# Two-block transformer step on one core: the last residual, norm, transposes and first feed-forward products by token tiles, the last stores by 512 columns

## The chip, the cores and the metric

The kernel runs as one program on one core of a Trainium2 chip. The metric is the device time of one execution in microseconds (us). The engines are named as in the profile: PE (TensorE, with PEld for its weight loads), DVE (VectorE), ACT (ScalarE), POOL (GpSimd) and SP (SyncE, which issues most DMAs). Each engine executes its own instructions in order; waits on other engines go by semaphores.

## The reference, cut to what matters

A first block (a recurrent mixer, a dense feed-forward, a block attention and a mixture of experts) runs on 256 tokens of width 1024, and its result x enters a second block of two layers, modulated by a condition c. In layer 1, the last, the mixer is a latent attention whose result is projected by `od_w_o` (1024 x 1024). The part that the change touches is the end of that layer:

```python
def modulate(h, shift, scale):
    return h * (1 + scale) + shift

def conv_ffn(h, w_up, conv_w, conv_b, w_down):      # w_up 1024 x 5632, w_down 2816 x 1024
    u = dwconv_centred(h @ w_up, conv_w, conv_b)     # over 3 neighbouring tokens
    a, g = jnp.split(u, 2, axis=-1)
    return (a * jax.nn.silu(g)) @ w_down
...
        yx, yc = odd_mixer(...)                      # ends in (...) @ w_o
        x = x + g1 * rms_norm(yx, norm_g[l, 1])
        hx = modulate(rms_norm(x, norm_g[l, 2]), sh2, sc2)
        x = x + g2 * rms_norm(conv_ffn(hx, ffn_w_up[l], ...), norm_g[l, 3])
    return x
```

All weights and activations are float32.

## The kernel before

**Tiles.** The 256 tokens are two token tiles of 128 (`tb` 0 and 1). A matrix lies either by tokens (tokens on the 128 partitions, `h`, `ypr`, `ffy`) or transposed (128 of the 1024 features on the partitions, all 256 tokens along the row, 8 blocks k, as `hT0h`). `h` is the residual stream, `ypr` the output projection's result, `ffy` first the normed rows and later the feed-forward's result.

**Products.** A float32 product is made of three products in the format f32r: each operand is split in a high part (suffix h, `whi`) and the rest (suffix l, `wlo`), and high by high, low by high and high by low are summed in PSUM (`mm`, L312). `wload` brings a weight panel by DMA into `wraw` (six buffers), ACT copies it to `whi` (L297) and DVE subtracts for `wlo` (L300, 128x512 at a time).

**Stages.** Generators yield after each step and a scheduler, which also orders the instructions of each engine, interleaves them. `x_chain` runs layer 1 in this order: `mla_x` (attention), `out_proj`, `modulated`, `ffn_conv`, and with its end the program ends.

- `lin_tok` (L378 and following) multiplies by tokens, 512 columns of the result at a time, with operand `omla` for the projection. In the last column block it holds back the last two groups of weights and finishes tile 0 before tile 1; after tile 0 it calls `late()`, by which `gate_row` makes the gate vector `gcol` into a row on all partitions (`brow`).
- `residual` (L1453) runs after the whole projection, for tile 0 and then tile 1: squares of `ypr` on ACT (`sq`), the sum (`ss`) and the scale (`rp`) on DVE, the root on POOL (`rs`, L343), two products with the gate row, and two `stt` (L309) of 512 columns that add to `h`.
- `modulated` (L1428) works out `scale` and `shift` (8 columns each), norms both tiles to `ffy` (`inv_rms` and L304), and calls `to_T`. That transposes on PE, 16 pieces of 128x128 (`tr`, L332, weights are the identity), two feature blocks of both tiles in one PSUM tile, applies scale and shift in pieces of 256 tokens (`hT0h` and `tT`), and splits into `hT0h` and `hT0l`.
- `ffn_parts` (L934) goes through the 2816 hidden features in units of 256. A unit loads a panel of 256 columns of the gate half, makes its 48 products (`mmT`: 8 blocks, 3 products, 2 column tiles; the weight panel is the loaded side, the 256 tokens move), and the same for the up half: 96 products of 256 moving columns with 128x128 weights. `unit` applies the convolution (`cv`) and the gate. After 12 and again after 10 of the 22 column tiles `lin_tok` multiplies by `w_down`.
- The last `lin_tok` calls `late()` for the gate row, then a last `residual` runs over both tiles, and after each tile a store of 128 x 1024 (512 KB) leaves on SP's queue (L2055).

Of the kernel before, what the change touches and what calls it, by code (L numbers as in the profile page):

```python
# [11 lines left out]
AF = mybir.ActivationFunctionType  # L12
# [4 lines left out]
P = 128  # L17
# [219 lines left out]
class Net:  # L237
# [136 lines left out]
    def lin_tok(self, ch, x, nk, src, n, evac, ntb=2, mt=P, late=None):  # L374

        for c0 in range(0, n, 512):
            ncol = min(512, n - c0)  # L380
            acc = [self.ps(ch) for _ in range(ntb)]

            def step(k0, w, tbs):
                m = min(4, nk - k0)
                for p0 in range(0, m, w.per):
                    ks = range(k0 + p0, k0 + min(m, p0 + w.per))
                    for lo in range(2):
                        for tb in tbs:
                            sl = slice(tb * mt, tb * mt + mt)
                            o = acc[tb][:mt, :ncol]  # L390
                            for k in ks:
                                if lo:
                                    self.mm(o, x.hi(k)[:, sl], w.lo(k - k0), False, k == nk - 1)
                                else:
                                    self.mm(o, x.hi(k)[:, sl], w.hi(k - k0), k == 0, False)
                                    self.mm(o, x.lo(k)[:, sl], w.hi(k - k0), False, False)
            k0s = list(range(0, nk, 4))
            held = k0s[-LATE:] if late is not None and c0 + 512 >= n else []
            ws = []
            for k0 in k0s:  # L400
# [43 lines left out]
    def to_T(self, ch, src, x, nk=KD, scale=None, bias=None, f32=None):  # L444

        for k0 in range(0, nk, 2):
# [12 lines left out]
            else:  # L459
# [434 lines left out]
def rwkv_out(N, st, ch=0):  # L894

    nc, a = N.nc, N.a
    h = N.slot(0, "h1")
    nc.scalar.dma_start(h.rearrange("p (b c) -> p b c", b=2), a["x"][0].rearrange("(b p) c -> p b c", p=P))
    x = st["yT"]

    def evac(c0, ncol, tb, p):
        o = h[:, tb * D + c0:tb * D + c0 + ncol]
        N.stt(o, o, ALPHA, p[:, :ncol], ALU.mult, ALU.add)
    yield from N.lin_tok(ch, x, KD, a["rwkv_w_out"], D, evac, late=lambda: None)
    N.layer_norm(lambda tb: h[:, tb * D:(tb + 1) * D], (0, 0), lambda tb: h[:, tb * D:(tb + 1) * D])
    st["h"] = h
    yield
# [23 lines left out]
        return self._v((k // 2) * 4 + 2 + k % 2, 1)  # L931


def ffn_parts(N, ch, x, wa, wg, parts, slots, unit, evac, wdown, late=None):  # L934
# [21 lines left out]
def ffn_dense(N, st, ch=0):  # L956
# [14 lines left out]
    def evac(part, c0, ncol, tb, p):  # L971
# [3 lines left out]
        else:  # L975
            N.tt(o, o, p[:, :ncol], ALU.add)
    yield from ffn_parts(N, ch, x, a["ffn_w_gate"], a["ffn_w_up"], (12, 10), (4, 5, 6), unit, evac, a["ffn_w_down"],
                         lambda: None)
# [48 lines left out]
def moba(N, st, ch=0):  # L1027
# [65 lines left out]
    yield from paced(N.lin_tok(ch, o, KD, a["moba_w_o"], D, evac, late=lambda: None), SIDE["moba_out"])  # L1093
# [331 lines left out]
    return rs  # L1425


def modulated(N, st, ch, src, l, which, r, slots, scr):  # L1428

    q = 3 * which  # L1430
    sc = N.sm(8, "scale")
    N.ts(sc, st["mod"].piece(l, q + 1, r), 1.0, op0=ALU.add)
    N.tt(sc, sc, N.v["norm_g_2"][:, (l * 4 + 2 * which) * 8:(l * 4 + 2 * which) * 8 + 8], ALU.mult)
    sh = N.sm(8, "shift")
    N.nc.vector.tensor_copy(sh, st["mod"].piece(l, q, r))
    for tb in range(2):
        s = slice(tb * D, (tb + 1) * D)
        rs = inv_rms(N, src[:, s])
        N.ts(scr[:, s], src[:, s], rs)
    x = N.act_slots(slots[0], slots[1], f"hT{ch}")  # L1440
    N.to_T(ch, lambda tb: scr[:, tb * D:(tb + 1) * D], x, scale=sc, bias=sh)
    return x


def gate_row(N, st, ch, l, which, r):
# [4 lines left out]
    return bcast_row(N, ch, col)  # L1450


def residual(N, x, y, row, done=None):  # L1453

    for tb in range(2):
        s = slice(tb * D, (tb + 1) * D)
        rs = inv_rms(N, y[:, s])
        for j in range(2):
# [2 lines left out]
        for j in range(2):  # L1461
            q = slice(tb * D + j * 512, tb * D + (j + 1) * 512)
            N.stt(x[:, q], y[:, q], rs, x[:, q], ALU.mult, ALU.add)
        if done is not None:
            done(tb)


def store_evac(N, y):
# [2 lines left out]
    return evac  # L1471


def ffn_conv(N, st, ch, src, l, r, x, hslots, parts, y, done=None):

    a = N.a
    cw, cb = N.v["ffn_conv_w_2"], N.v["ffn_conv_b_2"]
# [21 lines left out]
    def evac(part, c0, ncol, tb, p):  # L1499
# [3 lines left out]
        else:  # L1503
            N.tt(o, o, p[:, :ncol], ALU.add)
    up = a[f"ffn2_up{l}"]
    row = []
    yield from ffn_parts(N, ch, x, up[:, 0:FF], up[:, FF:2 * FF], parts, hslots, unit, evac, a[f"ffn2_down{l}"],
                         lambda: row.extend(gate_row(N, st, ch, l, 1, r)))
    residual(N, src, y, row, done)
    yield  # L1510


# [330 lines left out]
    st["yx_act"] = o  # L1843


def out_proj(N, st, ch, o, w, src, l, r, yslot):
    y = N.slot(yslot, f"ypr{ch}")
    row = []
    yield from N.lin_tok(ch, o, KD, w, D, store_evac(N, y), late=lambda: row.extend(gate_row(N, st, ch, l, 0, r)))
    residual(N, src, y, row)  # L1850
    yield


# [180 lines left out]
def x_chain(N, st, out, ch=0):  # L2034
# [34 lines left out]
def paced(g, n):  # L2069
    for _ in g:  # L2070
        yield n
# [49 lines left out]
```

## Time and profile before

| | us |
|---|---|
| median of 3 runs | 2861.41 |
| lowest and highest | 2859.16, 2861.59 |
| the profiled execution | 2861.41 |
| its span in the profile | 2859.6 |
| PE busy | 2754.8 (96%) |
| PEld busy | 2263.5 (79%) |
| DVE busy | 2210.2 (77%) |
| ACT busy | 1774.7 (62%) |
| POOL busy | 67.0 (2%) |

All rows come from the profiled execution, whose time is 1.8 us longer than its span. A row of a timeline is a group of equal instructions that follow one another: its start counted from the span's start, the time from its first start to its last end, and their number. Products of PE overlap in the array, so that a single one shows longer than the distance between the starts of two.

### The profile page before, as it was taken

The page shows a single profiled execution, that of the slowest core. Times are in us where ns is not written, and L with a number is a line of the kernel's source. Part 1 is how long each engine was busy: PE and PEld are TensorE (multiplying, and loading weights), DVE is VectorE, ACT ScalarE, POOL GpSimd, SP SyncE. Part 2 cuts the span into 40 slices and gives each one's busy share as a digit, 9 for nine tenths or more (in the row PEclk, how much of TensorE's full clock was granted, in tenths as well). Part 3 has the DMA queues.
Part 4 walks back from the last instruction along what each step waited for, and adds up shares of the span by engine and source line. Part 5 has one row for each costly group of instructions (what it writes and reads, how often), then busy time and mean ns, then how long its engine had stood idle before and what let it go on. Part 6 is the DMA issues. An engine that isn't in the chain of part 4 may idle for free. (4 is left out here: it accounts for less than half of the span.)

```text
span 2859.6 us, 49921 instructions
## 1 busy us (share of the span) xinstructions
PE 2754.8 (96%) x18356; PEld 2263.5 (79%) x18356; DVE 2210.2 (77%) x4350; ACT 1774.7 (62%) x3603; POOL 67.0 (2%) x87
## 2 busy tenths in 40 slices
PE   8999899999999999999999999989989999989898
PEld 8677589897866777777778777768877899877897
DVE  7356385677587989998998899987687787886767
ACT  5223264444566887778787878766546665666654
POOL 0011100000000000000000000000000000000000
PEclk9999999999999999999999999989999999999999
DMA  7444655544439999999999999965443465421453
GB/s 250 157 149 153 218 193 181 180 137 138 150 107 331 359 333 353 348 358 334 347 363 341 346 349 362 353 248 175 159 137 114 133 198 180 155 78 45 148 185 125
DMA packets 183662, 641.15 MB, mean 224 GB/s; under 512 B 22737, under 2 KB 28241, under 8 KB 183410
## 3 DMA queue, kind: packets, MB, share of 16 engines
q1 hardware_dynamic: 175200, 625.58, 62.7%
q10 hardware_dynamic: 8210, 12.30, 1.4%
q8 instruction: 146, 2.39, 0.3%
q14 instruction: 106, 0.87, 0.1%
HBM read 636.76 MB, written 1.05 MB: 223 GB/s over the span
## 5 line engine op out<-in xcount | busy, mean ns | idle before, releaser
L300 DVE TENSOR_TENSOR wlo<-wraw,whi 128x512 fp32r<-128x512 f32 (+1 forms) x2181 | 1375.7, 684 | 312.8 <-ACT whi L297 249.1
L297 ACT ACTIVATE whi<-wraw 128x512 fp32r<-128x512 f32 (+1 forms) x2181 | 1212.9, 621 | 418.2 <-PE ps L312 318.6
L312 PE MATMUL ps<-whi,xg 128*128 128x512 f32 x1792 | 497.2, 397 | 1.4 <-ACT whi L297 1.4
L312 PEld LDWEIGHTS ps<-whi,xg 128*128 128x128 f32 x1792 | 327.2, 188 | 83.4 <-ACT whi L297 22.3
L312 PE MATMUL ps<-wlo,xg 128*128 128x512 f32 x896 | 294.1, 399 | 0.4
L312 PE MATMUL ps<-whi,hT 128*128 128x512 f32 x896 | 259.9, 400 | 0.0
L312 PE MATMUL ps<-hT0h,whi 128*128 128x256 f32 (+2 forms) x872 | 216.7, 286 | 3.8 <-ACT whi L297 3.3
L312 PE MATMUL ps<-hT0l,whi 128*128 128x256 f32 (+2 forms) x872 | 216.7, 285 | 0.1
L312 PEld LDWEIGHTS ps<-wlo,xg 128*128 128x128 f32 x896 | 168.2, 188 | 53.6 <-DVE wlo L300 17.9
L312 PE MATMUL ps<-whi,hid 128*128 128x512 f32 x704 | 190.4, 406 | 10.3 <-DVE cv L309 7.1
L312 PEld LDWEIGHTS ps<-whi,hT 128*128 128x128 f32 x896 | 164.5, 188 | 31.9
L312 PEld LDWEIGHTS ps<-hT0h,whi 128*128 128x128 f32 (+2 forms) x872 | 168.2, 193 | 4.9 <-ACT whi L297 3.5
L312 PEld LDWEIGHTS ps<-hT0l,whi 128*128 128x128 f32 (+2 forms) x872 | 168.3, 193 | 0.9 <-DVE hT0l L300 0.4
L312 PE MATMUL ps<-wlo,hT 128*128 128x512 f32 x448 | 168.0, 415 | 0.0
L312 PEld LDWEIGHTS ps<-whi,hid 128*128 128x128 f32 x704 | 131.7, 191 | 45.0 <-issue 15.6
L312 PE MATMUL ps<-hT1h,whi 128*128 128x256 f32 (+1 forms) x504 | 127.9, 290 | 12.0 <-ACT whi L297 11.4
L309 DVE SCALAR_TENSOR_TENSOR cv<-ps,vecs,cv 128x255 f32<-128x255 f32 x264 | 124.6, 479 | 12.7 <-ACT cv L297 11.3
L312 PE MATMUL ps<-hT1l,whi 128*128 128x256 f32 (+1 forms) x504 | 125.9, 286 | 0.0
L312 PE MATMUL ps<-hT0h,wlo 128*128 128x256 f32 (+2 forms) x872 | 123.9, 283 | 1.6 <-DVE wlo L300 1.5
L312 PEld LDWEIGHTS ps<-hT0h,wlo 128*128 128x128 f32 (+2 forms) x872 | 112.9, 191 | 2.8 <-DVE wlo L300 2.4
L312 PEld LDWEIGHTS ps<-wlo,hT 128*128 128x128 f32 x448 | 84.1, 188 | 30.7 <-DVE wlo L300 14.0
L312 PEld LDWEIGHTS ps<-hT1h,whi 128*128 128x128 f32 (+1 forms) x504 | 96.5, 192 | 14.9 <-ACT whi L297 13.5
(528 smaller groups left out, 4475.1 us busy)
## 6 DMA issues: line engine op xcount, KB each, us to landing
wraw<-moe_w_down SPq DMA_DIRECT2D x224, 512.0 KB, 5.5
wraw<-moe_w_gate SPq DMA_DIRECT2D x222, 512.0 KB, 5.1
wraw<-moe_w_up SPq DMA_DIRECT2D x222, 512.0 KB, 5.3
wraw<-ffn_up SPq DMA_DIRECT2D x132, 512.0 KB, 3.7
wraw<-ada_w SPq DMA_DIRECT2D x96, 512.0 KB, 4.6
wraw<-ffn_down SPq DMA_DIRECT2D x66, 512.0 KB, 4.0
wraw<-ffn_w_gate SPq DMA_DIRECT2D x22, 512.0 KB, 4.0
wraw<-ffn_w_up SPq DMA_DIRECT2D x22, 512.0 KB, 3.5
```

The source lines that it names most:

```text
L297: self.nc.scalar.activation(out, in_, f, **kw)
L300: (eng or self.nc.vector).tensor_tensor(out, x, y, op=op)
L309: (eng or self.nc.vector).scalar_tensor_tensor(out, x, s, y, op0=op0, op1=op1)
L312: self.nc.tensor.matmul(out, l, r, start=start, stop=stop)
```

## The change

`lin_tok` calls `late(tb)` after each of the two token tiles and no longer only after tile 0. `out_proj` takes a function `then`; where it is given, the residual of a token tile, and behind it the norm, the transposes and the splits of that tile (`Modulated.tile`, `to_T_tile`), are written into the program directly behind the tile's last product of the projection. `to_T_tile` puts four feature blocks of one tile in one PSUM tile, applies scale and shift in pieces of 128 tokens, even blocks on ACT and odd ones on DVE, and splits 512 elements at a time. The normed activations get the slots 8 and 9 in place of 2 and 3, and the PSUM tiles come from the other pool.

In the first unit of this feed-forward `ffn_parts` loads the panels of both halves and then makes, for tile 0 and then tile 1, all its products with 128 moving columns: 192 in place of 96. The other units are as before. The last residual is called by tiles from `late(tb)`, and a store of 128 x 512 (256 KB) leaves after each `stt`. The calls of `lin_tok` in other stages only take the new argument.

```diff
@@ lin_tok
                 evac(c0, ncol, tb, acc[tb])
-                if tb == 0:
-                    late()
+                late(tb)
                 yield
...
+    def to_T_tile(self, ch, src, tb, x, scale, bias):
+        for k0 in range(0, KD, 4):
+            p = self.ps(ch)
+            t = self.t512("tT")
+            for k in range(4):
+                self.tr(p[:, k * P:(k + 1) * P], src[:, (k0 + k) * P:(k0 + k + 1) * P])
+            for k in range(4):
+                o = slice(k * P, (k + 1) * P)
+                g, b = scale[:, k0 + k:k0 + k + 1], bias[:, k0 + k:k0 + k + 1]
+                if k % 2:
+                    self.ts(t[:, o], p[:, o], g, b, ALU.mult, ALU.add)
+                else:
+                    self.act(t[:, o], p[:, o], AF.Identity, scale=g, bias=b)
+            h, l = (z[:, k0 * T:(k0 + 4) * T].rearrange("p (k t) -> p k t", k=4)[:, :, tb * P:(tb + 1) * P] for z in (x.h, x.l))
+            self.split(h, l, t.rearrange("p (k t) -> p k t", k=4))
...
@@ ffn_parts
-            for w in (wa, wg):
+            if tiles and c0 == 0:
+                wts = [N.wload(w[:, 0:256], KD, 256) for w in (wa, wg)]
+                ws = [N.ps(ch) for _ in wts]
+                for tb in range(2):
+                    xt = Act(lambda k: x.hi(k)[:, tb * P:(tb + 1) * P], lambda k: x.lo(k)[:, tb * P:(tb + 1) * P])
+                    for wt, acc in zip(wts, ws):
+                        for t in range(2):
+                            N.mmT(acc[:, t * T + tb * P:t * T + (tb + 1) * P], wt, xt, KD, t * P, t * P + P)
+                    yield
+            for w in () if ws else (wa, wg):
...
+class Modulated:
...
+    def norm(self, tb):
+        s = slice(tb * D, (tb + 1) * D)
+        rs = inv_rms(self.N, self.src[:, s])
+        self.N.ts(self.scr[:, s], self.src[:, s], rs)
+        return self.scr[:, s]
...
+    def tile(self, tb, ch):
+        self.N.to_T_tile(ch, self.norm(tb), tb, self.x, self.sc, self.sh)
...
@@ residual
-        if done is not None:
-            done(tb)
+            if done is not None:
+                done(tb, j)
...
@@ out_proj
+    def late(tb):
+        if tb == 0:
+            row.extend(gate_row(N, st, ch, l, 0, r))
+        if then is not None:
+            residual(N, src, y, row, (tb,))
+            then(tb)
...
@@ x_chain
-    yield from out_proj(N, st, ch, st["ox_act"], a["od_w_o_2"], h, 1, 0, 4)
     y = N.slot(12, "ffy1")
-    x = modulated(N, st, ch, h, 1, 1, 0, (2, 3), y)
-    yield
-    yield from ffn_conv(N, st, ch, h, 1, 0, x, (4, 5, 6), (12, 10), y,
-                        lambda tb: nc.sync.dma_start(out[tb * P:(tb + 1) * P], h[:, tb * D:(tb + 1) * D]))
+    m = Modulated(N, st, ch, h, 1, 1, 0, (8, 9), y)
+    def then(tb):
+        if tb == 0:
+            m.begin()
+        m.tile(tb, 1 - ch)
+    yield from out_proj(N, st, ch, st["ox_act"], a["od_w_o_2"], h, 1, 0, 4, then)
+    yield
+    def store(tb, j):
+        c = slice(j * 512, (j + 1) * 512)
+        nc.sync.dma_start(out[tb * P:(tb + 1) * P, c], h[:, tb * D + j * 512:tb * D + (j + 1) * 512])
+    yield from ffn_conv(N, st, ch, h, 1, 0, m.x, (4, 5, 6), (12, 10), y, store, True)
```

The order of PE behind the output projection, in the kernel before (`omlah` is the projection's operand, `ident` the transposes' identity; 16 transposes serve both tiles):

```order
L312 MATMUL ps<-wlo,omlah 128x512 x2
L332 MATMUL ps<-ident,ffy_39342 128x128 x16
L312 MATMUL ps<-hT0h,whi 128x256
L312 MATMUL ps<-hT0l,whi 128x256
L312 MATMUL ps<-hT0h,whi 128x256
```

And in the changed kernel, at the same place, from the last of tile 0's products that stand ahead of tile 1's transposes (`ps<-ident` stands for them):

```order
L312 MATMUL ps<-hT0h,whi 128x128
L312 MATMUL ps<-hT0l,whi 128x128
L312 MATMUL ps<-hT0h,wlo 128x128 x4
L332 MATMUL ps<-ident,ffy_39131 128x128 x8
L312 MATMUL ps<-hT0h,wlo 128x128 x4
```

Behind tile 0's 8 transposes stand 21 of its 96 products of 128 columns (9 of `hT0h` by `whi`, 8 of `hT0l` by `whi`, 4 by `wlo`), then tile 1's 8 transposes, then the other 75 and the 96 of tile 1; the units of 256 columns follow.

The order of DVE in the kernel before, from tile 1's sum to the norm of both tiles (`ypr` by `brow` is the product with the gate row):

```order
L300 TENSOR_TENSOR ypr_39131<-ypr_39131,brow 128x512
L306 TENSOR_SCALAR rp<-ss 128x1
L300 TENSOR_TENSOR wlo<-wraw,whi 128x512
L309 SCALAR_TENSOR_TENSOR h_4135<-ypr_39131,rs,h_4135 128x512 x2
L304 TENSOR_SCALAR scale<-modT 128x8
```

And in the changed kernel, from tile 0's norm to tile 1's residual:

```order
L304 TENSOR_SCALAR ffy_39131<-h_4135,rs 128x1024
L300 TENSOR_TENSOR wlo<-wraw,whi 128x512 x2
L306 TENSOR_SCALAR tT<-ps,scale,shift 128x128
L300 TENSOR_TENSOR wlo<-wraw,whi 128x512
L306 TENSOR_SCALAR tT<-ps,scale,shift 128x128
L300 TENSOR_TENSOR ypr_39137<-ypr_39137,brow 128x512
L306 TENSOR_SCALAR tT<-ps,scale,shift 128x128 x2
L300 TENSOR_TENSOR ss<-ss 128x1
L300 TENSOR_TENSOR ypr_39137<-ypr_39137,brow 128x512
L300 TENSOR_TENSOR hT0l<-tT,hT0h 128x4x128 x2
L306 TENSOR_SCALAR rp<-ss 128x1
L309 SCALAR_TENSOR_TENSOR h_4135<-ypr_39137,rs,h_4135 128x512 x2
```

Tile 0's norm, its four pieces of scale and shift and its two splits now stand ahead of tile 1's `rp`; between the ends of the two residuals there are 8 weight splits ahead of that `rp`, one more than the 7 before. The orders of all engines ahead of the projection's end and behind the first unit are otherwise as before, but for the stores, two neighbours that change places on PE in the projection, and the vectors `scale` and `shift`, which are worked out in the attention's last steps.

## Rows read from the trace of the kernel before

**Rows 1.** The page: span, and busy us (share) xinstructions.
```profile
span 2859.6 us, 49921 instructions
...
PE 2754.8 (96%) x18356; PEld 2263.5 (79%) x18356; DVE 2210.2 (77%) x4350; ACT 1774.7 (62%) x3603; POOL 67.0 (2%) x87
```

**Rows 2.** Chain of waits, end of the program: start us, us, what.
```profile
2661.19 190.07 PE ps L312 x1323
```

**Rows 3.** PE's timeline around the first unit: start, us, instructions [idle before <-releaser].
```profile
2647.45 0.61 PE L312 MATMUL ps<-wlo,omlah 128*128 128x512 f32 x2
2655.50 1.09 PE L332 MATMUL ps<-ident,ffy 128*128 128x128 f32 x4 [7.43 <-DVE ss L300]
2657.14 2.82 PE L332 MATMUL ps<-ident,ffy 128*128 128x128 f32 x12 [0.56 <-DVE ffy L304]
2660.46 0.58 PE L312 MATMUL ps<-hT0h,whi 128*128 128x256 f32 x1 [0.49 <-DVE tT L306]
...
2661.57 0.41 PE L312 MATMUL ps<-hT0h,whi 128*128 128x256 f32 x1
2661.78 0.41 PE L312 MATMUL ps<-hT0l,whi 128*128 128x256 f32 x1
...
2673.26 1.12 PE L312 MATMUL ps<-hT0h,wlo 128*128 128x256 f32 x8
2674.22 0.28 PE L312 MATMUL ps<-hT0h,whi 128*128 128x256 f32 x1
```

**Rows 4.** Windows of the gap: busy us of each engine, granted clock, DMA.
```profile
core 0: us, PE busy (x) PEld busy (x) DVE busy (x) ACT busy (x) POOL busy (x), PEclk, DMA share, GB/s
2648.00:2651.00 3.00, 0.07 (x1) 0.00 (x0) 3.00 (x8) 3.00 (x9) 0.00 (x0) 1.00 0.81 247
2651.00:2655.50 4.50, 0.00 (x0) 0.03 (x1) 3.33 (x11) 1.51 (x6) 1.40 (x2) 0.51 0.82 300
2660.40:2664.70 4.30, 4.09 (x17) 3.80 (x18) 3.14 (x6) 2.85 (x6) 0.00 (x0) 0.50 0.00 0
2664.70:2674.20 9.50, 9.50 (x81) 9.50 (x80) 3.87 (x8) 4.34 (x9) 0.00 (x0) 1.00 0.22 62
```

**Rows 5.** DVE's timeline in the gap.
```profile
2644.59 1.41 DVE L309 SCALAR_TENSOR_TENSOR h<-ypr,rs,h 128x512 f32<-128x512 f32 x2
2645.92 4.29 DVE L300 TENSOR_TENSOR wlo<-wraw,whi 128x512 fp32r<-128x512 f32 x7
...
2650.80 0.15 DVE L306 TENSOR_SCALAR rp<-ss 128x1 f32<-128x1 f32 x1
...
2651.99 1.42 DVE L309 SCALAR_TENSOR_TENSOR h<-ypr,rs,h 128x512 f32<-128x512 f32 x2 [0.45 <-POOL rs L343]
...
2655.27 0.15 DVE L300 TENSOR_TENSOR ss<-ss 128x1 f32<-128x1 f32 x1
...
2656.33 0.76 DVE L304 TENSOR_SCALAR ffy<-h,rs 128x1024 f32<-128x1024 f32 x1 [0.65 <-POOL rs L343]
2658.68 1.72 DVE L306 TENSOR_SCALAR tT<-ps,scale,shift 128x256 f32<-128x256 f32 x3 [1.60 <-ACT hT0h L297]
```

**Rows 6.** ACT's timeline in the gap.
```profile
2653.44 0.63 ACT L297 ACTIVATE sq<-h 128x512 f32<-128x512 f32 x1
```

**Rows 7.** 128-column products in layer 0: PE's timeline, then their ns min/median/max.
```profile
555.37 1.05 PE L312 MATMUL ps<-mlqk 128*128 128x128 f32 x8
...
L312 PE MATMUL ps<-mlqk x64: 270/275/275, 555.4 to 2113.9; 128*128 128x128 f32 x64
```

**Rows 8.** Weight loads ahead of the experts: PEld's timeline.
```profile
880.27 0.53 PEld L312 LDWEIGHTS ps<-gates,moe_work 128*128 128x128 f32 x4
880.64 0.29 PEld L332 LDWEIGHTS ps<-ident,moe_work 128*128 128x128 f32 x2
880.90 0.53 PEld L312 LDWEIGHTS ps<-gates,moe_work 128*128 128x128 f32 x4
```

**Rows 9.** DMA issues at the end: KB each, median us to landing.
```profile
out<-h SPq DMA_DIRECT2D x2, 512.0 KB, 2.6
```

More of the change, by code (lines that the diff above doesn't have):

```diff
@@ L903, in evac @@
         N.stt(o, o, ALPHA, p[:, :ncol], ALU.mult, ALU.add)
-    yield from N.lin_tok(ch, x, KD, a["rwkv_w_out"], D, evac, late=lambda: None)
+    yield from N.lin_tok(ch, x, KD, a["rwkv_w_out"], D, evac, late=lambda tb: None)
     N.layer_norm(lambda tb: h[:, tb * D:(tb + 1) * D], (0, 0), lambda tb: h[:, tb * D:(tb + 1) * D])
@@ L931, in lo, with ffn_parts @@
         return self._v((k // 2) * 4 + 2 + k % 2, 1)
-def ffn_parts(N, ch, x, wa, wg, parts, slots, unit, evac, wdown, late=None):
+def ffn_parts(N, ch, x, wa, wg, parts, slots, unit, evac, wdown, late=None, tiles=False):
     k0 = 0
@@ L977, in ffn_dense @@
     yield from ffn_parts(N, ch, x, a["ffn_w_gate"], a["ffn_w_up"], (12, 10), (4, 5, 6), unit, evac, a["ffn_w_down"],
-                         lambda: None)
+                         lambda tb: None)
     N.layer_norm(lambda tb: h[:, tb * D:(tb + 1) * D], (0, 1), lambda tb: h[:, tb * D:(tb + 1) * D])
@@ L1092, in evac @@
         N.stt(q, q, ALPHA, p[:, :ncol], ALU.mult, ALU.add)
-    yield from paced(N.lin_tok(ch, o, KD, a["moba_w_o"], D, evac, late=lambda: None), SIDE["moba_out"])
+    yield from paced(N.lin_tok(ch, o, KD, a["moba_w_o"], D, evac, late=lambda tb: None), SIDE["moba_out"])
     N.layer_norm(lambda tb: h[:, tb * D:(tb + 1) * D], (1, 0), lambda tb: h[:, tb * D:(tb + 1) * D])
@@ L1425, in inv_rms, with __init__, begin @@
     return rs
-def modulated(N, st, ch, src, l, which, r, slots, scr):
[L1430 to L1435, printed above, removed]
-    for tb in range(2):
[L1437 to L1442, printed above, removed]
+class Modulated:
+    def __init__(self, N, st, ch, src, l, which, r, slots, scr):
+        q = 3 * which
+        self.N, self.ch, self.src, self.scr = N, ch, src, scr
+        self.sc = N.sm(8, "scale")
+        N.ts(self.sc, st["mod"].piece(l, q + 1, r), 1.0, op0=ALU.add)
+        N.tt(self.sc, self.sc, N.v["norm_g_2"][:, (l * 4 + 2 * which) * 8:(l * 4 + 2 * which) * 8 + 8], ALU.mult)
+        self.sh = N.sm(8, "shift")
+        N.nc.vector.tensor_copy(self.sh, st["mod"].piece(l, q, r))
+        self.slots = slots
+    def norm(self, tb):
[3 more added lines that the diff above has]
+        return self.scr[:, s]
+    def begin(self):
+        self.x = self.N.act_slots(self.slots[0], self.slots[1], f"hT{self.ch}")
+    def tile(self, tb, ch):
+        self.N.to_T_tile(ch, self.norm(tb), tb, self.x, self.sc, self.sh)
+def modulated(N, st, ch, src, l, which, r, slots, scr):
+    m = Modulated(N, st, ch, src, l, which, r, slots, scr)
+    for tb in range(2):
+        m.norm(tb)
+    m.begin()
+    N.to_T(ch, lambda tb: scr[:, tb * D:(tb + 1) * D], m.x, scale=m.sc, bias=m.sh)
+    return m.x
 def gate_row(N, st, ch, l, which, r):
@@ L1450, in gate_row, with residual @@
     return bcast_row(N, ch, col)
-def residual(N, x, y, row, done=None):
-    for tb in range(2):
+def residual(N, x, y, row, tiles=(0, 1), done=None):
+    for tb in tiles:
         s = slice(tb * D, (tb + 1) * D)
@@ L1471, in store_evac, with ffn_conv @@
     return evac
-def ffn_conv(N, st, ch, src, l, r, x, hslots, parts, y, done=None):
+def ffn_conv(N, st, ch, src, l, r, x, hslots, parts, y, done=None, tiles=False):
     a = N.a
@@ L1506, in ffn_conv @@
     row = []
+    def late(tb):
+        if tb == 0:
+            row.extend(gate_row(N, st, ch, l, 1, r))
+        if done is not None:
+            residual(N, src, y, row, (tb,), done)
     yield from ffn_parts(N, ch, x, up[:, 0:FF], up[:, FF:2 * FF], parts, hslots, unit, evac, a[f"ffn2_down{l}"],
-                         lambda: row.extend(gate_row(N, st, ch, l, 1, r)))
-    residual(N, src, y, row, done)
+                         late, tiles)
+    if done is None:
+        residual(N, src, y, row)
     yield
@@ L1843, in even_x, with out_proj, late @@
     st["yx_act"] = o
-def out_proj(N, st, ch, o, w, src, l, r, yslot):
+def out_proj(N, st, ch, o, w, src, l, r, yslot, then=None):
     y = N.slot(yslot, f"ypr{ch}")
     row = []
-    yield from N.lin_tok(ch, o, KD, w, D, store_evac(N, y), late=lambda: row.extend(gate_row(N, st, ch, l, 0, r)))
-    residual(N, src, y, row)
+    def late(tb):
+        if tb == 0:
[3 more added lines that the diff above has]
+            then(tb)
+    yield from N.lin_tok(ch, o, KD, w, D, store_evac(N, y), late=late)
+    if then is None:
+        residual(N, src, y, row)
     yield
@@ L2049, in x_chain @@
     yield from mla_x(N, st, ch, x, dict(lat=4, q=(5, 6), k=(12, 7), v=13, o=(2, 3)))
-    yield from out_proj(N, st, ch, st["ox_act"], a["od_w_o_2"], h, 1, 0, 4)
     y = N.slot(12, "ffy1")
-    x = modulated(N, st, ch, h, 1, 1, 0, (2, 3), y)
+    m = Modulated(N, st, ch, h, 1, 1, 0, (8, 9), y)
+    def then(tb):
+        if tb == 0:
+            m.begin()
+        m.tile(tb, 1 - ch)
+    yield from out_proj(N, st, ch, st["ox_act"], a["od_w_o_2"], h, 1, 0, 4, then)
     yield
-    yield from ffn_conv(N, st, ch, h, 1, 0, x, (4, 5, 6), (12, 10), y,
-                        lambda tb: nc.sync.dma_start(out[tb * P:(tb + 1) * P], h[:, tb * D:(tb + 1) * D]))
+    def store(tb, j):
+        c = slice(j * 512, (j + 1) * 512)
+        nc.sync.dma_start(out[tb * P:(tb + 1) * P, c], h[:, tb * D + j * 512:tb * D + (j + 1) * 512])
+    yield from ffn_conv(N, st, ch, h, 1, 0, m.x, (4, 5, 6), (12, 10), y, store, True)
 def chain(*gens):
```

## The prediction

> **What bounds the kernel now.** I read the page's busy times first. TensorE (PE) is busy 2754.8 of 2859.6 us, 96%, VectorE (DVE) 77%, ScalarE (ACT) 62%; PE's weight loads run beside its products [rows 1]. The chain of waits then shows that from 2661.19 us on, PE's products alone carry the program for 190.07 us [rows 2]. What happens before that point and delays PE therefore reaches the end at full size, and what finds room beside PE is worth nothing. The change sits just ahead of this point, so the windows and PE's timeline come next.
>
> The output projection's last products start at 2647.45 and show until 2648.06. PE then waits 7.43 us for the residual and the norm of both token tiles, transposes (4 at 2655.50, 12 at 2657.14), waits again, and begins the feed-forward's first unit at 2660.46 [rows 3]. From 2648.06 to 2660.46 lie 12.4 us, of which the 16 transposes are some 3.9. The granted clock falls in this gap to 0.50, the lower level of 1.2 GHz, and is still there when the products begin; it is back at 1.00 (2.4 GHz) from about 2664.7 [rows 4]. At the lower level two products of 256 columns start 0.21 us apart; at the higher, eight take 1.12 us where one shows 0.28, which makes (1.12 - 0.28)/7 = 0.120 each [rows 3]. The second unit begins at 2674.22 [rows 3]. That is the mark for what follows: the forecast is by how much it moves.
>
> **The part that fills the gap.** Tile 0 no longer waits for tile 1. Its residual sum on DVE ends at 2644.59 + 1.41 = 2646.0 [rows 5], while the projection's last products still run. In the new order one product with the gate row less stands ahead of it (0.6 us), so it ends near 2645.4. Squares on ACT, the root on GpSimd (POOL) and the scaling follow between weight splits on DVE, and tile 0's 8 transposes can start near 2649.4 instead of 2655.50. So far the gap closes by 6 us.
>
> What PE can do with it is bounded by its queue, which is in order. The new order has behind tile 0's transposes only 21 of its 96 products, then tile 1's 8 transposes, and only then the other 75 and tile 1's 96. Whatever delays tile 1 stops all 171 of them.
>
> **The part that delays tile 1.** DVE worked without a break from tile 0's residual at 2644.59 to tile 1's norm scale (rp) at 2650.80 [rows 4, 5]. The new order puts tile 0's work ahead of it. I add it up from the residual's end at 2645.4: 8 weight splits at 4.29/7 = 0.61 make 4.9; the scaling 0.76; four scale-and-shift pieces of 128 columns, for which no row stands, between the 0.15 of one column and the 0.57 of 256 columns (1.72/3), so half-way 0.36, 1.4 together; two gate products and two hT0l splits at 0.6, 2.4; three sums over one column, about 0.4. That gives 2645.4 + 9.9 = 2655.3, against 2650.80 [rows 5]. From there to the transposes the path is the old one without tile 0's share: residual 1.19 us later, two squares that end at 2654.07 - 2650.80 = 3.3 us after rp [rows 6], then from the sum at 2655.27 to the transposes at 2657.14 another 1.9 [rows 3, 5]; with the step between, 5.2 us. Tile 1's transposes come at 2655.3 + 5.2 = **2660.5**, 3.4 us later than the 12 transposes at 2657.14. The 21 products of tile 0 are done by then, and PE stands idle for some 4 us.
>
> **The part that adds work to PE.** The first unit's 96 products of 256 columns become 192 of 128. Each still loads its own 128x128 weights. What that costs has two near rows. Products of plain f32 with 128 columns and 128x128 weights: eight take 1.05 us where one shows 0.275, (1.05 - 0.275)/7 = 0.111 each [rows 7]. Loads of 128x128 beside products of one column and short transposes: six start within 880.90 - 880.27 = 0.63 us, 0.105 each [rows 8]. So halving the columns hardly shortens a product: I take 0.112, near the first row, with 0.105 and 0.120 (the 256-column product) as ends. The unit then costs 192 x 0.112 = 21.5 us instead of 96 x 0.120 = 11.5, ten more. This alone is near the 12.4 us that a perfect filling of the gap could give, and the queue allows only 21 products of filling, 2.4 us at the higher clock.
>
> The Trainium skill speaks against 0.112: "TensorE: Matmul & The Clock Gate", section "Back-to-back issue gap", gives about 81 ns for a sustained stream of loads and products with 128 columns. The rows here are at 0.105 to 0.111 and no run of before has 0.081; with that figure for the 144 products at the higher clock in the sum below, the second unit would start at 2668.0 + 144 x 0.081 = 2679.7 and the time be 2866.3 us, which is among the rivals.
>
> **The sum.** Tile 1's transposes at 2660.5, at the lower clock (PE was idle before them, as before): 8 x 0.21 = 1.7, until 2662.2. Before, the clock was low for 7.5 us from the transposes at 2657.14 to about 2664.6; I let the same stretch follow 2660.5, until 2668.0. The 5.8 us left of it hold 5.8/0.21 = 27 products. The other 144 take 144 x 0.112 = 16.1. The second unit begins at 2684.1, against 2674.22: **+9.9 us**. From there the order on all engines is that of before, and PE alone sets the end.
>
> **The stores.** The two last stores of 512 KB take 2.6 us from issue to landing [rows 9]. Now the last one is 256 KB and the half before leaves one residual step (1.42/2 = 0.7 us) earlier. At the 300 GB/s with a share of 0.82 in the window at 2651 [rows 4], 512 KB take some 1.4 us, so half saves 0.7 at most and 0 at least, if the landing is all fixed time; I take **-0.6**, since the longer part is then data.
>
> **What I cost at nothing.** Scale and shift vectors are worked out earlier on DVE, three instructions of the size of rp's 0.15, in the attention's last rows where PE is ahead; if PE waited for them, 0.5. The normed activations lie in two other slots and the transposes use another accumulator pool; nothing on PE is queued for these. Weight panels of gate and up are loaded together, in the order on SyncE that stands there anyway; their splits on DVE end before tile 1's products need them, since PE stands at the transposes. The second unit's splits have the 16 us of the first unit's products as cover; without it, about 1 us of one split pair.
>
> The profiled execution took 2861.41 us, which is also the median of the three runs, and its span 2859.6; the 1.8 us outside stay. The forecast is 2861.41 + 9.9 - 0.6 = **2870.7 us**.
>
> **Rivals.**
> *The clock stays up.* PE's idle stretch is cut in two by tile 0's work, so the clock might be at 1.00 at 2660.5. Against it: it fell in the window from 2651.00 [rows 4], after some 3 us of idleness, and here about 1.5 and then 4 us stay. It would give 2660.5 + 8 x 0.112 + 171 x 0.112 = 2680.6, +6.4, and with the stores 2867.2.
> *The product is cheap, and the change is not slower.* If loads hide behind the products and a product goes by its columns, it costs half of 0.120 at the higher clock and 0.12 at the lower: 48 products in the low 5.8 us, the other 123 take 7.4, and the second unit begins at 2675.4, +1.2, with the stores 2862.0 us: no change. The place is the first unit's weight loads; it decides from a price of 0.087 down, where 2668.0 + 144 x 0.087 = 2680.5, or +5.7 with the stores. For it speaks that loads run beside products, as the busy times of both show [rows 1]; against it, both near rows [rows 7, 8]. A rival beside it is the price of the Trainium skill's section "Back-to-back issue gap": the 2866.3 above, no change either.
> *Tile 1 is not late.* If DVE takes tile 0's pieces in waits that the sum does not see, rp stays near 2652 and the transposes at 2657.1; everything shifts by 3.4, to 2867.3. Against it: DVE has no idle time there until 2651 [rows 4].
> *The product is dear.* If 128 columns of this number format cost as much as two 256-column products, 0.24, then 12 fit into the low 5.8 us, the other 159 take 38.2, the second unit begins at 2706.2, and the time is 2892.8. Against it is the row of plain f32.
>
> **How the numbers follow.** 0.2% is 5.7 us, about what a measurement of this kernel can tell from no change: same is 2855.7 to 2867.1. Main case 0.74, own range 2865 to 2874 (0.105: -1.0; 0.120: +1.2; transposes 1 us either way; the low clock 1.5 us shorter or longer: 0.8; stores +0.6; runs down to 2859.16: -2.2). Clock up 0.09, cheap 0.07 (0.03 of it at half the price, 0.04 between that and 0.087), tile 1 not late 0.04, dear 0.03, and 0.03 for what I do not see and count as faster. Slower gets the main case, the dear one and half of the two cases that end near 2867.2, less 0.05 for the main case's lower edge: 0.78; same 0.19. The range leaves out the dear case and most of the cheap one and reaches from 2864.0 to 2874.0.
>
> **What would show it.** In the profile of the changed kernel: tile 0's transposes near 2649.4; tile 1's near 2660.5, after some 4 us in which PE waits for DVE's scaling; products of 128 columns 0.105 to 0.12 us apart at the higher clock; the first 256-column products of the second unit near 2684. If products are under 0.09 apart, or tile 1's transposes stand before 2658, the forecast is too high; if the gap from 2648 to tile 1's transposes is filled, the in-order reading is wrong.

## The result and the profile after

The changed kernel takes 2886.17 us (median of 6 runs, 2881.15 to 2888.83) against 2860.16 us before (6 runs beside it): 1.0087 times as long, 95% interval 1.0077 to 1.0097, some 25 us. That is slower, as forecast, but by 2.7 times the forecast 9.3 us, and outside the range. The profiled execution took 2886.91 us, 25.5 more than that of before.

The page of the changed kernel, its span and busy times (compare [rows 1]), and the piece of its chain of waits that ends the program (start us, us, what; compare [rows 2]):

```profile
span 2885.1 us, 50121 instructions
...
PE 2785.3 (97%) x18452; PEld 2294.6 (80%) x18452; DVE 2210.8 (77%) x4354; ACT 1774.9 (62%) x3605; POOL 67.0 (2%) x87
```

```profile
2662.56 214.95 PE ps L312 x1399
```

PE is busy 30.5 us longer and the others as before, and the piece that PE carries alone is 24.9 us longer. PE's timeline of the changed kernel shows where (start, us, instructions [idle before <-releaser]; compare [rows 3]):

```profile
2649.94 1.06 PE L332 MATMUL ps<-ident,ffy 128*128 128x128 f32 x8 [1.81 <-DVE ffy L304]
2654.06 0.69 PE L312 MATMUL ps<-hT0h,whi 128*128 128x128 f32 x2 [3.06 <-ACT hT0h L297]
...
2660.62 1.94 PE L332 MATMUL ps<-ident,ffy 128*128 128x128 f32 x8 [1.12 <-DVE ffy L304]
...
2663.10 0.41 PE L312 MATMUL ps<-hT0h,whi 128*128 128x128 f32 x1
2663.32 0.41 PE L312 MATMUL ps<-hT0l,whi 128*128 128x128 f32 x1
...
2697.02 1.91 PE L312 MATMUL ps<-hT0h,wlo 128*128 128x128 f32 x8
2698.73 0.52 PE L312 MATMUL ps<-hT0h,whi 128*128 128x256 f32 x1
...
2703.36 0.28 PE L312 MATMUL ps<-hT0h,whi 128*128 128x256 f32 x1
```

Tile 0's transposes come at 2649.94, tile 1's at 2660.62, and then two products start 0.21 us apart, not for some 6 us but to the last one. The second unit begins at 2698.73 against 2674.22. The windows show the granted clock (seventh figure, PEclk; compare [rows 4]):

```profile
core 0: us, PE busy (x) PEld busy (x) DVE busy (x) ACT busy (x) POOL busy (x), PEclk, DMA share, GB/s
2660.40:2664.70 4.30, 4.08 (x20) 4.11 (x20) 1.81 (x6) 2.43 (x6) 0.00 (x0) 0.50 0.00 0
2664.70:2674.20 9.50, 9.50 (x47) 9.50 (x46) 1.15 (x2) 0.41 (x1) 0.00 (x0) 0.50 0.01 2
2674.20:2699.20 25.00, 25.00 (x118) 25.00 (x119) 5.28 (x10) 5.96 (x11) 0.00 (x0) 0.50 0.14 43
...
2698.70:2703.30 4.60, 4.60 (x26) 4.60 (x26) 3.72 (x8) 1.13 (x2) 0.00 (x0) 0.58 0.50 154
```

Before, the clock was back at 1.00 from 2664.7 on. Here PE is busy without a break from 2663 to 2699 and the clock stays at 0.50; it comes back 4 us after the second unit's products of 256 columns have begun. On DVE, tile 1's scale and its norm, and the last residual (compare [rows 5]):

```profile
2655.65 0.15 DVE L306 TENSOR_SCALAR rp<-ss 128x1 f32<-128x1 f32 x1
...
2659.72 0.75 DVE L304 TENSOR_SCALAR ffy<-h,rs 128x1024 f32<-128x1024 f32 x1 [0.65 <-POOL rs L343]
...
2880.65 1.42 DVE L309 SCALAR_TENSOR_TENSOR h<-ffy,rs,h 128x512 f32<-128x512 f32 x2 [0.75 <-POOL rs L343]
```

The account closes. The second unit begins 24.5 us later. Its first 24 products take 2703.36 - 2698.73 = 4.63 us at the low clock in place of 24 x 0.120 = 2.88, 1.75 more. From the last residual to the end of the span it is 2885.1 - 2880.65 = 4.45 us against 2859.6 - 2854.39 = 5.21 before, 0.76 less. 24.5 + 1.75 - 0.76 = 25.5, the whole difference of the two profiled executions.

### The profile page after: what moved, and what is told of

It reads as the page before. It is cut to its first block, busy times and chain, and to the rows that moved or that the text cites. A ratio compares the mean times of both kernels' runs of the same rounds, so it can differ in the third digit from the quotient of the medians.

```text
span 2885.1 us, 50121 instructions
## 1 busy us (share of the span) xinstructions
PE 2785.3 (97%) x18452; PEld 2294.6 (80%) x18452; DVE 2210.8 (77%) x4354; ACT 1774.9 (62%) x3605; POOL 67.0 (2%) x87
## 5 line engine op out<-in xcount | busy, mean ns | idle before, releaser
L312 PE MATMUL ps<-hT0h,whi 128*128 128x256 f32 (+1 forms) x904 | 234.7, 294 | 6.6 <-ACT whi L297 3.5
L312 PE MATMUL ps<-hT0l,whi 128*128 128x256 f32 (+1 forms) x904 | 234.7, 294 | 0.4 <-DVE hT0l L300 0.4
L312 PEld LDWEIGHTS ps<-hT0h,whi 128*128 128x128 f32 x904 | 182.6, 202 | 7.8 <-ACT whi L297 3.9
L312 PEld LDWEIGHTS ps<-hT0l,whi 128*128 128x128 f32 x904 | 182.9, 202 | 1.1 <-DVE hT0l L300 0.6
L312 PE MATMUL ps<-hT0h,wlo 128*128 128x256 f32 (+1 forms) x904 | 135.9, 294 | 1.3 <-DVE wlo L300 1.2
L312 PEld LDWEIGHTS ps<-hT0h,wlo 128*128 128x128 f32 x904 | 124.5, 202 | 2.7 <-DVE wlo L300 2.2
```

Source lines behind the costliest of these rows:

```text
L312: self.nc.tensor.matmul(out, l, r, start=start, stop=stop)
```

## The experiments

Times differ by up to 0.5% from run to run, and the stage begins up to 7.5 us earlier or later in one trace than in that of before, so I compare one distance: from the start of the projection's last product (0.23 us behind the start of the group of two that ends it) to the start of the second unit. It is 26.5 us before and 51.0 after. The kernel with only its stores changed, whose order is that of before up to the end, has 26.7, so steps of some tenths of a us mean nothing.

| kernel | distance, us | against before, us | time against before, 95% interval |
|---|---|---|---|
| before | 26.5 | | |
| changed kernel | 51.0 | +24.5 | 1.0087 (1.0077 to 1.0097) |
| its first unit by 256 columns | 30.2 | +3.7 | 1.0006 (0.9996 to 1.0017) |
| before, first unit by 128 columns | 54.3 | +27.8 | 1.0098 (1.0081 to 1.0115) |
| the same, up half alone by 128 | 31.5 | +5.0 | 1.0015 (1.0006 to 1.0025) |
| first unit by 128, filling that ends early | 56.7 | +30.1 | 1.0109 (1.0094 to 1.0124) |
| first unit by 256, filling that ends early | 29.4 | +2.8 | 1.0010 (0.9999 to 1.0021) |
| first unit by 128, filling up to the unit | 52.6 | +26.0 | 1.0118 (1.0103 to 1.0133) |
| first unit by 128, more filling | 37.4 | +10.8 | 1.0042 (1.0028 to 1.0056) |
| changed kernel with filling | 35.2 | +8.7 | 1.0029 (1.0019 to 1.0039) |

**One part undone: the first unit in wide products.**

```diff
-    yield from ffn_conv(N, st, ch, h, 1, 0, m.x, (4, 5, 6), (12, 10), y, store, True)
+    yield from ffn_conv(N, st, ch, h, 1, 0, m.x, (4, 5, 6), (12, 10), y, store)
```

> The changed kernel with the first unit in products of 256 columns again (96, in place of 192 of 128); residual, norm and transposes stay by token tiles, the stores by 512 columns. Theory N (a stream of 128-column products does not bring the clock back): tile 1's transposes stay near 2660.6, the products of the first unit begin near 2664, the clock is back some 4 us later as it was before, and the second unit begins near 2677.8, 3.6 us later than before; with the stores about 2863, ratio 1.001. Theory S (tile 0's early pieces and the two idle stretches hold the clock down, whatever the width): the 96 products go at 0.21 us each, the second unit begins near 2684.5, and the time is near 2870.

Median 2863.82 against 2861.29 us. PE's timeline of this kernel, in which the stage begins 1.92 us later than before:

```profile
2662.47 1.94 PE L332 MATMUL ps<-ident,ffy 128*128 128x128 f32 x8 [9.61 <-DVE ffy L304]
2666.41 0.80 PE L312 MATMUL ps<-hT0h,whi 128*128 128x256 f32 x2 [2.00 <-ACT hT0h L297]
...
2678.85 1.12 PE L312 MATMUL ps<-hT0h,wlo 128*128 128x256 f32 x8
2679.81 0.28 PE L312 MATMUL ps<-hT0h,whi 128*128 128x256 f32 x1
```

Tile 1's transposes stand at 2662.47 - 1.92 = 2660.55, as in the changed kernel, and the idle stretch ahead of them is longer (9.61 us), yet the clock is back in the unit, which ends at the full pitch. So neither tile 1's delay nor the broken start holds the clock down. What is left of the change without narrow products costs 3.7 us at the unit, about tile 1's delay of 3.5.

**One part alone: the first unit in narrow products.**

```diff
+            if c0 == tiles:
+                wts = [N.wload(w[:, c0:c0 + 256], KD, 256) for w in (wa, wg)]
...
+                            N.mmT(acc[:, t * T + tb * P:t * T + (tb + 1) * P], wt, xt, KD, t * P, t * P + P)
...
+            for w in () if ws else (wa, wg):
```

> The kernel before with nothing but the first unit in 192 products of 128 columns; residual, norm and transposes of both tiles stand as before. Theory N: the clock, low at the unit's start at 2660.5, stays low to its end, 192 x 0.213 = 41.0, and the second unit begins near 2701.4, +27 us, 2887. Theory S: the start is that of before, the clock is back near 2664.7, the rest go at 0.112, and the second unit begins near 2684, +10 us, 2870.

Median 2890.22 us. Two windows of its first unit, and the second unit's start in PE's timeline:

```profile
2670.00:2680.00 10.00, 10.00 (x49) 10.00 (x48) 0.00 (x0) 0.00 (x0) 0.00 (x0) 0.50 0.01 2
2680.00:2690.00 10.00, 10.00 (x49) 10.00 (x48) 0.00 (x0) 0.00 (x0) 0.00 (x0) 0.50 0.00 0
```

```profile
2704.43 0.52 PE L312 MATMUL ps<-hT0h,whi 128*128 128x256 f32 x1
```

PE has no idle time and the clock stays at 0.50 to the end of the unit. The narrow products alone make the loss, and more of it (27.8) than the whole change, which starts some of them early.

**The same unit shape in a place where the clock is full.** The edit is the one above with `tiles` = 768, the fourth unit.

> The kernel before with the fourth unit of the last feed-forward (hidden columns 768 to 1023) in 192 products of 128 columns; they begin with the clock at its full level and PE busy for 25 us. Theory N: the products start 0.11 us apart; if the width alone decides, the clock then falls within the unit and they go on 0.21 apart, between +9.8 (never falls) and +29 us. Theory S: the clock stays, 192 x 0.111 against 96 x 0.120, +9.8 us, 2870. Theory F (this number format costs 0.213 us with 128 columns at any clock): 0.213 apart from the first one on with the granted clock at 1.00, 41.0 against 11.5, +29.5 us, 2889.7.

Median 2870.78 against 2861.29 us, ratio 1.0034 (1.0022 to 1.0046). A window in the middle of that unit, PE's rows at the unit's start and there, and the start of the next unit:

```profile
2710.00:2715.00 5.00, 5.00 (x48) 5.00 (x46) 0.00 (x0) 0.00 (x0) 0.00 (x0) 1.00 0.00 0
```

```profile
2701.75 0.22 PE L312 MATMUL ps<-hT0h,whi 128*128 128x128 f32 x1
...
2711.53 1.06 PE L312 MATMUL ps<-hT0h,wlo 128*128 128x128 f32 x8
...
2723.15 0.33 PE L312 MATMUL ps<-hT0h,whi 128*128 128x256 f32 x1
```

From 2701.75 to 2723.15 the 192 products take 21.4 us, 0.1115 each, with the clock at 1.00 throughout. The theory that this format costs 0.213 at any clock falls, and so does the one that narrow products always bring the clock down. The price of 0.112 in the prediction was right. The Trainium skill's 81 ns ("TensorE: Matmul & The Clock Gate", section "Back-to-back issue gap") isn't reached by these products; the measured 0.1115 decides.

**Half of the unit narrow, behind the wide half.** As the first-unit edit, with `N.mmT(ws[0][:, t * T:(t + 1) * T], wts[0], x, KD, t * P, t * P + P)` for the gate half.

> The kernel before with only the up half of the first unit in products of 128 columns (96 of them, 6 among the first 22 products and 90 behind the 48 of 256 columns of the gate half). Theory N2: the wide products bring the clock back near 2665 as before and the narrow ones keep it, 96 x 0.112 against 48 x 0.120, +5 us, 2865. If narrow products at this place cost 0.21 at any rate (theory P): 96 x 0.213 against 5.8, +14.7 us, 2875.

Median 2865.33 us. The windows of the narrow half:

```profile
2673.00:2677.00 4.00, 4.00 (x37) 4.00 (x35) 0.55 (x1) 2.04 (x4) 0.00 (x0) 1.00 0.01 4
2677.00:2687.00 10.00, 10.00 (x92) 10.00 (x91) 4.21 (x9) 3.08 (x7) 0.00 (x0) 1.00 0.33 105
```

Products that are mostly wide (13 of the first 17) bring the clock back first, near 2672.3, the narrow ones behind them keep it, and the distance grows by the 5.0 us that the pitch of 0.112 gives. The place isn't to blame.

**Filling that ends before the unit.** In the next experiments PE does products that nobody reads, so that it isn't idle ahead of the unit.

```diff
+    if warm:
+        p = N.ps(1 - ch)
+        for _ in range(warm):
+            N.mm(p, N.ident, N.cc[:, 0:512], True, True)
     residual(N, src, y, row)
```

> The kernel before with the first unit in 192 products of 128 columns, and with 14 products of 512 plain f32 columns, whose result nobody reads, behind the output projection (some 0.44 us each, 6.2 us, in the 7.4 us that PE waits for tile 0's norm). Theory N2 (a stream of 128-column products keeps the level of the clock that it begins with, and only a stream of wider products raises it): the clock is full at the transposes and stays so, 192 x 0.112 = 21.5 us for the unit, 16 transposes in half the time; about +9 us against before, 2870, and 20 less than the same kernel without the filling products. Theory P (the place decides: the products behind the norm are slow when they are narrow, for their operands or their weights, and the clock only follows): 0.21 apart again, 2888.

> The kernel before with nothing but the 14 filling products of 512 columns behind the output projection. Theory N2: the clock stays full through the gap; the 12 transposes behind the norm take 1.4 in place of 2.8 us and the first products 0.12 in place of 0.21; the second unit begins 2 to 3.3 us earlier, 2857 to 2858.5, ratio 0.9988 to 0.9993. Theory P: as before, 2860; if the filling products end after tile 0's norm, up to 1 us more.

I had the filling's size wrong: one such product shows as two rows that start 0.43 us apart, so 14 took 12.0 us in place of 6.2, and the unit began 2.7 us later than before. Medians 2892.09 with the narrow unit, and 2863.61 (ratio 1.0010, 0.9999 to 1.0021) with the wide one, against 2861.62. Windows of the kernel with the narrow unit, from its first product on:

```profile
2661.00:2662.50 1.50, 1.01 (x5) 0.72 (x6) 1.50 (x4) 1.50 (x4) 0.00 (x0) 1.00 0.00 0
2662.50:2663.20 0.70, 0.70 (x7) 0.62 (x6) 0.70 (x2) 0.67 (x2) 0.00 (x0) 0.91 0.00 0
2663.20:2665.00 1.80, 1.80 (x10) 1.80 (x9) 0.79 (x2) 0.26 (x1) 0.00 (x0) 0.50 0.00 0
```

The clock was still full when the narrow products began, some of them waiting for operands, and then fell among them. "Narrow products keep the level that they meet" is therefore too simple, and the next two runs ask under which condition. The kernel with the wide unit and the same filling shows that the fall is not a matter of narrow products:

```profile
2661.70:2663.10 1.40, 0.98 (x4) 0.64 (x5) 1.40 (x4) 1.40 (x4) 0.00 (x0) 1.00 0.00 0
2663.10:2664.00 0.90, 0.90 (x6) 0.90 (x6) 0.88 (x2) 0.87 (x2) 0.00 (x0) 0.55 0.00 0
2664.00:2666.50 2.50, 2.50 (x13) 2.50 (x13) 0.69 (x1) 0.15 (x1) 0.00 (x0) 0.50 0.02 7
2666.50:2670.00 3.50, 3.50 (x31) 3.50 (x30) 0.00 (x0) 1.07 (x3) 0.00 (x0) 0.99 0.00 0
```

Its clock falls at the same place, behind the idle stretch of 1.31 us and the waits of its first products, but is back some 3.4 us later. What the narrow unit lacks is the return: its clock stays at 0.50 from 2663.1 until the second unit's wide products.

**Filling up to the unit.** 8 products in the gap and, behind the last transposes:

```diff
+    p = N.ps(1 - ch)
+    for _ in range(3):
+        N.mm(p[:, 0:512], N.ident, y[:, D:D + 512], True, True)
```

> The kernel before with the first unit in 192 products of 128 columns and filling products that reach up to it: 8 of 512 plain f32 columns behind the output projection (two passes of 0.435 each, 7.0 us), 3 of 512 columns of the normed rows behind the last transposes (2.6 us). Theory N2 (narrow products hold the level that they meet): the clock is at 1.00 when the first narrow product starts, and the unit takes 192 x 0.112 = 21.5 us at 1.00 throughout; the second unit near 2683, +9 us, about 2870. Theory N3 (narrow products at the start of a stage bring the clock down by themselves, as it fell at 2663.2 in the kernel whose filling ended 3 us earlier): the clock falls within the first 5 us and the unit goes on at 0.213, second unit near 2699, about 2887.

Median 2892.98 us. The profiled execution, 2883.30, is the fastest of its four (the others took 2891.67 to 2896.33), so its distance in the table, +26.0, is less than the 32 us between the medians. Windows of its first unit:

```profile
2657.00:2658.00 1.00, 0.99 (x8) 0.77 (x7) 0.80 (x2) 0.45 (x1) 0.00 (x0) 1.00 0.00 0
2658.00:2659.00 1.00, 0.77 (x7) 0.77 (x7) 0.17 (x1) 0.00 (x0) 0.00 (x0) 1.00 0.00 0
2659.00:2660.00 1.00, 1.00 (x11) 1.00 (x10) 0.00 (x0) 0.00 (x0) 0.00 (x0) 0.92 0.08 16
2660.00:2661.00 1.00, 1.00 (x7) 1.00 (x6) 0.00 (x0) 0.00 (x0) 0.00 (x0) 0.50 0.00 0
```

The first products come 7 or 8 to the us where a stream without waits has 9, since they wait for their splits. Just behind them the clock falls, now in a stream without gaps, and doesn't come back before the wide products. Theory N2 fails here; N3 and one in which the waits count both fit. With `range(6)` in place of `range(3)` all operands are there when the unit may start:

> The kernel before with the first unit in 192 products of 128 columns and more filling behind the last transposes than in the run before: 6 products of 512 columns (5.2 us) in place of 3, so that all operands of the unit are ready when its first product may start, and no product waits. Theory N4 (narrow products hold the full clock where they follow one another without a gap, and lose it where they wait between them): the clock stays at 1.00 to the unit's end, 192 x 0.112 = 21.5 us; with the filling's delay of some 2.6 us the second unit comes about 12 us later than before, 2873. Theory N3 (narrow products at the start of a stage bring it down by themselves): it falls within the unit, 2888 to 2892.

Median 2871.89 against 2860.67 us. The window over the unit, and PE's row at its end:

```profile
2660.00:2682.00 22.00, 22.00 (x198) 21.93 (x197) 4.99 (x10) 5.34 (x11) 0.00 (x0) 1.00 0.14 46
```

```profile
2681.45 0.34 PE L313 MATMUL ps<-hT0h,whi 128*128 128x256 f32 x1
```

The same 192 products at the same place now go at the full clock to the last. So the narrow start alone does not bring it down (N3 falls); it fell where waits stood between the first products. That the waits and not the longer filling itself decide is the likeliest reading of these two runs, but both differ between them, so it stays argued. Nor do waits alone decide: the wide unit of the last kernel below, behind 1.3 us less filling, waits 0.33 and 0.34 us at its first products and keeps the full clock.

**The changed kernel with filling.** 3 products behind tile 0's transposes and 3 that read tile 1's residual, ahead of tile 1's transposes.

```diff
+            m.tile(0, 1 - ch)
+            fill(p, y[:, 0:512], 3)
+        else:
+            fill(p, h[:, D:D + 512], 3)
+            m.tile(1, 1 - ch)
```

> The changed kernel with filling products of 512 plain f32 columns: 3 behind tile 0's transposes (2.6 us) and 3 that read tile 1's residual, ahead of tile 1's transposes (2.6 us). 8 of tile 0's products remain ahead of tile 1's transposes, 184 behind. Theory N2: the clock is at 1.00 at tile 1's transposes near 2660.6, they take 0.9, and 184 x 0.112 = 20.6 brings the second unit to 2682; with the stores some 7 us more than before, 2868, and 18 less than the changed kernel. Theory N3: the clock falls behind the transposes, and the time is that of the changed kernel, 2886.

Median 2868.55 against 2861.00 us. PE's rows around tile 1's transposes (the stage begins 1.7 us later than in the changed kernel) and windows:

```profile
2659.01 4.51 PE L313 MATMUL ps<-h,ident 128*128 128x512 f32 x6 [1.16 <-DVE h L310]
2663.36 1.04 PE L333 MATMUL ps<-ident,ffy 128*128 128x128 f32 x8
```

```profile
2659.00:2663.40 4.40, 4.39 (x7) 1.81 (x8) 1.66 (x5) 1.28 (x4) 0.55 (x1) 0.61 0.00 0
...
2670.00:2684.00 14.00, 14.00 (x128) 14.00 (x128) 4.25 (x8) 4.18 (x8) 0.00 (x0) 1.00 0.16 45
```

The clock fell about 2659, and the wide filling brought it back within 4.4 us, in which PE would else have been idle or at narrow work; from there on 184 narrow products held it. Six products that nobody reads take 16 of the 24.5 us away. This is the test of the changed kernel's own loss.

**The stores alone**, by 512 columns:

```diff
-        if done is not None:
-            done(tb)
+            if done is not None:
+                done(tb, j)
```

> The kernel before with nothing but the stores by 512 columns. All theories: the order of the products is that of before, the last store is half as long, 0.6 us less (0 to 0.7), so 2859.6 against 2860.2; less than the runs scatter, so it is read from the time between the last residual step and the end of the span.

Median 2861.92, ratio 1.0002 (0.9991 to 1.0013): nothing that runs can tell. In its trace the last residual starts at 2856.52 and the span is 2861.0, 4.48 us against 5.21:

```profile
2856.52 1.41 DVE L309 SCALAR_TENSOR_TENSOR h<-ffy,rs,h 128x512 f32<-128x512 f32 x2 [0.75 <-POOL rs L343]
```

So 0.73 us are gained, under the scatter of the runs. The other traces bear it out: from the last residual to the end it is 4.5 us in each of the six with stores of 256 KB, and 5.2 in each of the eight with stores of 512 KB.

**Attempts at a faster kernel.** The first keeps the units wide and has the early-ending filling, transposes by tiles behind both norms, and the stores:

> The kernel before with the 14 filling products, with the transposes by token tiles behind both norms (the residual's and the norm's order on VectorE is that of before, so tile 1 is not delayed), products of 256 columns, and the stores by 512 columns. Sum of the parts if they are independent: 2 to 3.3 us from the clock, 0.5 from the transposes, since tile 0's scale and shift run under tile 1's norm, 0.7 from the stores: 3.2 to 4.5 us less than before, 2856 to 2857, ratio about 0.9986. If the pieces of 128 columns cost ScalarE and VectorE more than they save on PE, 1 us less gain.

Median 2863.32 against 2861.62, ratio 1.0010 (0.9999 to 1.0020), no gain. PE's first product of the unit waits longer than in the kernel with filling alone, where that wait is 1.31 us, and ACT's split releases it; that the pieces of four blocks by 128 columns keep ACT and DVE busy ahead of it is argued:

```profile
2668.68 0.80 PE L313 MATMUL ps<-hT0h,whi 128*128 128x256 f32 x2 [3.13 <-ACT hT0h L298]
```

The second leaves the transposes as before, and has the stores and filling up to the unit (8 in the gap, 3 of 256 columns behind the transposes):

> The kernel before with the stores by 512 columns and filling products up to the first unit: 8 of 512 plain f32 columns behind the output projection (7.0 of the 7.4 us of waiting), 3 of 256 columns behind the last transposes (1.3 us); all units in products of 256 columns. Theory N2: the clock stays at 1.00; transposes in half the time, the first 20 products 0.12 apart, second unit near 2672 in place of 2674.2; with the stores 2.9 us less, ratio 0.999. Theory N3: the same, since no product here is narrow but the transposes. If the filling delays the first product, up to 1 us less gain.

Median 2860.51 against 2861.00, ratio 0.9994 (0.9983 to 1.0005). Its distance is 25.1 us, 1.4 less than before, with the clock at 1.00 in the first unit:

```profile
2660.80:2664.00 3.20, 2.85 (x19) 2.51 (x20) 2.91 (x5) 2.35 (x5) 0.00 (x0) 1.00 0.00 0
```

With the 0.7 of the stores that makes 2.1 us less, not the expected 2.9, as the first products now wait for their splits; the runs don't separate it from before. No version here is shown to be faster than the kernel before.

## Why the prediction was right and wrong

- *What bounds, and that a delay passes to the end*: right. 24.5 us at the second unit and 1.75 behind it are found again at the end.
- *Tile 0 early*: transposes forecast near 2649.4, measured 2649.94.
- *Tile 1 late*: rp forecast 2655.3, measured 2655.65; transposes forecast 2660.5, measured 2660.62. The sum over DVE's queue, worked out from rows of before and the new order, held to 0.4 us. The 3.7 us of the kernel with wide products are about this term alone.
- *The price of a narrow product*: forecast 0.112 at the full clock, measured 0.1115 in the fourth unit; at the low clock 0.21, as taken. That "no run of before has 0.081" holds for 128x128 weights only: with weights of 64 columns the trace of before has 16 products of 128 columns 0.055 us apart.

```profile
2164.81 1.09 PE L312 MATMUL ps<-R,nk_nav 128*64 128x128 f32 x16
```

- *The clock, the step that failed.* "I let the same stretch follow 2660.5, until 2668.0" took the low stretch of before, which ended some 4 us after the wide products had begun, as a time that passes after PE begins to work, whatever it works on; the unit's narrow products do not end it. Here they filled the window 2663.0 to 2698.7 and it did not end. The 144 products that were put at 0.112 took 0.2135: 144 x 0.1015 = 14.6 us, which is 24.5 - 9.9. The low clock in the second unit, 1.75 us, follows from it.
- *The rivals*: the one on the clock looked only to the side on which it stays up. That it stays down as long as products are narrow, with a price from the rows at hand (171 x 0.21 = 36, second unit near 2698, 2885 us), was not among them, though [rows 4] had no stretch in which narrow products had raised the clock; that was the gap in the reading. The dear product came near the time by another mechanism, which the fourth unit refutes.
- *The stores*: -0.6 forecast, -0.76 measured.
- *Costed at nothing*: nothing of it shows; 24.5 + 1.75 - 0.76 leaves no rest.

## What to carry to other kernels

Halving the moving columns of a product that loads 128x128 weights halves its work, not its time: 0.1115 against 0.120 us here, so a unit split by token tiles costs nearly twice, and the gap that it should fill has to be larger than that. A first stage behind an idle stretch should begin with wide products: the same split cost 10 us more where the clock was up and 28 where it was down. When a forecast takes over a low-clock stretch from the trace, ask what PE did when the clock came back, and whether the changed kernel does that too.

## What was not expected of the hardware

A stream of f32r products with 128 columns and 128x128 weights, 0.2135 us apart and without a gap, left the granted clock at 0.50 for 35.7 us in the changed kernel. So it did for the whole first unit where this was the only change, and in two kernels with filling from the fall near its start to the unit's end. Products of 256 columns brought the clock back 2.3 to 6.3 us after their first one in each kernel where it was low at this place. At 1.00 the same narrow stream, 0.1115 apart, held it for 21 us (fourth unit), 20 us (changed kernel with filling) and 21.8 us (more filling). Behind waits of some tenths of a us at the unit's start the clock fell in two kernels with a narrow unit, but also in one with a wide unit.

128 columns alone are not the reason. Early in the trace of before, PE makes products of 128 columns with 64x64 weights at the low clock, 0.11 us apart, and four transposes between them, no wider product, and near 128.6 the clock is back:

```profile
124.98 1.97 PE L312 MATMUL ps<-wkvd,wkvd 64*64 64x128 f32 x16 [0.57 <-DVE wkvd L300]
126.89 1.11 PE L332 MATMUL ps<-ident,adar 128*128 128x128 f32 x4
127.93 1.41 PE L312 MATMUL ps<-wkvd,wkvd 64*64 64x128 f32 x16
```

```profile
125.20:128.60 3.40, 3.40 (x26) 2.74 (x26) 1.77 (x6) 0.00 (x0) 0.20 (x1) 0.50 0.00 0
128.60:132.00 3.40, 3.40 (x75) 2.88 (x73) 1.18 (x3) 0.94 (x3) 0.00 (x0) 1.00 0.02 5
```

These products differ from the unit's in their weights and in their format (plain f32), and no run here parts the two. The Trainium skill ("TensorE: Matmul & The Clock Gate", section "What's actually happening") has a kernel of 128 columns leave the lower level after some 49 products and says that the number of products doesn't count; the 171 products behind tile 1's transposes in the changed kernel, which did not leave it, disagree.

A product of plain f32 with 512 columns shows as two rows that start 0.43 us apart (28 rows for the 14 filling products), nearly four times the 0.23 of an f32r product in all. So the 128-column f32 rows [rows 7] that gave the price are most likely halves and not whole products; an f32r product then measured 0.1115 all the same, so this agreement is in part luck.
